# Rotation tables made in pieces during the recurrent phase and reloaded from device memory

## The chip, the cores and the metric

The kernel runs on one core of a Trainium2 chip. The metric is device time in microseconds (us) of one execution; the time before is the median of three. PE is TensorE (PEld its weight loads), DVE is VectorE, ACT is ScalarE, POOL is GpSimd, and SP is SyncE, which here only issues transfers.

## The reference, cut to what matters

One residual block over 2048 positions of width 1024: a norm, one projection to eight groups of 1024 columns, a recurrent branch and an attention branch over 8 heads, a merge by gates, an output projection and a final norm. The change touches the rotation of queries and keys by position, which concerns the first 32 of each head's 128 dimensions (16 frequencies, two halves).

```python
def apply_partial_rope(t, cos, sin):
    tf = t.astype(jnp.float32)
    half = ROT_DIM // 2
    x1 = tf[..., :half]
    x2 = tf[..., half:ROT_DIM]
    return jnp.concatenate([x1 * cos - x2 * sin, x2 * cos + x1 * sin, tf[..., ROT_DIM:]], axis=-1)
...
    inv_freq = ROPE_THETA ** (-jnp.arange(0, ROT_DIM, 2, dtype=jnp.float32) / ROT_DIM)
    ang = positions.astype(jnp.float32)[..., None] * inv_freq
    cos = jnp.cos(ang)[:, :, None, :]
    sin = jnp.sin(ang)[:, :, None, :]
...
        proj = h @ w_in[l]
        x_rnn, z_rnn, q, k, v, z_attn, g_r, g_a = jnp.split(proj, IN_SPLITS, axis=-1)
...
        qh = apply_partial_rope(q.reshape(B, S, N_HEADS, HEAD_DIM), cos, sin)
        kh = apply_partial_rope(k.reshape(B, S, N_HEADS, HEAD_DIM), cos, sin)
```

## The kernel before, in words

The positions are worked in two halves, f = 0 and 1, each of 1024 positions (two banks of 512, a tile being 128 columns of the projection by 512 positions). In each half come first the norm and the operands of the projection, with the values; then 28 pairs of column blocks are projected by Strassen's scheme (`strassen`): seven products of twelve 128 x 512 matmuls each, into PSUM tiles X (two of them), Z, W, V and Y (one each). Every matmul is three in float32 parts, hi and lo. A product `prod` takes its weight block S, split into hi and lo. In half 0 the block is made on the spot: SP loads raw blocks R (ring of five), DVE adds and subtracts them (L255 to L263), ACT writes hi (L200), POOL writes lo (L160), ACT's queue stores the result to memory (sD), and S is a ring of seven. In half 1 SP only loads it back (L288, 512 KB). The last product of a pair, into V, runs behind the first one of the next pair. Finished tiles are evicted through `done`: ACT or DVE (L418) writes them to an SBUF tile.

`prod` counts the products in `n_prod`. Code that should come some products later is put under a count in `late` or `after_prod`, and `prod` runs what is due; this gives the program's order. A planner then orders each engine's instructions, ahead of the run, from that order and its own estimate of when each is ready, so that an instruction can come earlier on its engine than its place in the program.

The pairs of a half form two phases. In the recurrent phase (buffers `rp`) eight pairs feed the recurrence (`recurrent`: steps tap, taps, split, gates, sigmoids, decay and so on to store, L735 to L834), and between them run pairs whose gates are evicted to a ring of three tiles "ev" and stored (`gate_pairs`), and two plain pairs. In the rotary phase (buffers `qp`) the rotation's tables are made, half 0 loads and normalises x for the next half (L468 to L478) and half 1 works out the residual gate, then two rotated pairs (one of queries, one of keys) and the remaining plain pairs run. A rotated pair holds the 32 rotated dimensions of all heads. Its four tiles go through `rotated`: eviction to t0 (three such in half 0, five in half 1), shuffle of the halves to t1 on DVE (L903), t0 times the cosine table Ct on POOL (L904), t1 times the signed sine table St on DVE (L905), the sum on DVE (L906), and four stores on SP (L909). Plain tiles are stored by SP too (L933).

`rotary_tables` makes Ct and St, each 128 x 1024, at the start of the rotary phase. It loads the half's positions, 8 per partition (`pi`, L838), and multiplies them by 16 frequencies to a tile `an` of 128 x 128. In 25 small DVE operations it brings the angles to within one turn by subtracting multiples of 2 pi in 8 and 5 parts (L849 to L853), makes the cosine's angle `co` a quarter turn further (L857, L858) and clips both (L860). Two ACT sines follow (L861). Then, for each bank and each of co and an, a DVE copy repeats the 4 x 8 x 16 values (`rep`, L868, one buffer), four PE transposes turn them (L870) to a PSUM tile pg (two of them, shared with the recurrent gates and the norm's transposes), and ACT (Ct, L874) or DVE (St, with a sign, L876) evicts 512 columns of the table. All on-chip; nothing of it goes to memory.

After both halves comes the attention, whose order is written out by hand, and which the change leaves alone.

Of the kernel before, what the change touches and what calls it, by code (L numbers as in the profile page):

```python
# [10 lines left out]
F32 = mybir.dt.float32  # L11
F32R = mybir.dt.float32r
BF16 = mybir.dt.bfloat16
I32 = mybir.dt.int32
AF = mybir.ActivationFunctionType
ALU = mybir.AluOpType
# [4 lines left out]
P = 128  # L21
# [3 lines left out]
NB = 4  # L25
CH = 512
H = 8
KH = KT // 2
HALF = 1024
# [5 lines left out]
FILL = (3.6, 3.1)  # L35
MORE = 0.8
NEG = 1e30

KV = 4

# [5 lines left out]
K_ID, K_QM, K_SG, K_IF, K_M23, K_M1, K_REP = 0, 128, 132, 133, 261, 773, 1029  # L46
# [4 lines left out]
def constants():  # L51
# [10 lines left out]
    old, prev, diag = q4, (d <= 0) + q4, np.where(d >= 0, 1 + q4, 0)  # L62
    add = np.array([NEG, 0.0, -math.log(2.0)])
    cst[:, K_M23 : K_M23 + 512] = add[np.concatenate([old, old, prev, diag], axis=1)]
# [6 lines left out]
def split_const(v, bits, n):  # L71
    out = []
    r = np.longdouble(v)
    for _ in range(n):
        m, e = math.frexp(float(r))
        q = math.floor(m * 2 ** bits) / 2 ** bits
        c = math.ldexp(q, e)
        out.append(c)
        r = r - np.longdouble(c)
    return out  # L80


TWO_PI = 8 * np.arctan(np.longdouble(1))
# [3 lines left out]
def decoder_block(ctx, tc, x, c, positions, g_norm, w_mod, b_mod, w_in, b_gate, conv_w, conv_b,  # L87
                  w_a, b_a, w_x, b_x, lam, w_out_rnn, w_out_attn, w_o, g_final, cst, out):
    nc = tc.nc
    cnt = [0]  # L90

    def T(pool, shape, dt, tag, **kw):
        cnt[0] += 1
        return pool.tile(shape, dt, tag=tag, name=f"{tag}_{cnt[0]}", **kw)
# [3 lines left out]
    def scratch(name, shape):  # L98
        return nc.dram_tensor(name, shape, F32, kind="Internal").ap()
# [10 lines left out]
    oT = scratch("oT", [D, S])  # L110
    meT = scratch("meT", [D, S])
    gateD = scratch("gateD", [1, D])

    sD = scratch("sD", [28 * 7, P, 2, KH, P])

# [20 lines left out]
    cs = T(cp, [P, N_CST_A], F32, "cs")  # L136
    ident = cs[:, K_ID : K_ID + P]
# [68 lines left out]
    n_prod, late, after_prod = [0], {}, {}  # L206
# [205 lines left out]
    def total(dst, ps, u, perm=lambda ap: ap):  # L412

        with tc.high_priority():
            if u is None:
                nc.scalar.activation(dst, perm(ps[:]), AF.Copy)
            else:
                nc.vector.tensor_tensor(dst, perm(ps[:]), perm(u[:]), ALU.add)  # L418
# [20 lines left out]
    def wcol(c0, n=P):  # L439
        return w_in[0, :, c0 : c0 + n]  # L440
# [17 lines left out]
    pg = pools.open("pg", bufs=2, space=PSUM)  # L458
# [107 lines left out]
    pt = T(pg, [P, CH], F32, "pg")  # L566
# [30 lines left out]
    for j in range(4):  # L597
# [3 lines left out]
        with ExitStack() as order:  # L601
            for ins in pm_ins[-1:] + gs_ins[-2:-1] + acc_ins[-1:]:
                order.enter_context(tc.issue_after(ins))
            for q in range(2):
                t = w_m[q, j]
# [227 lines left out]

        strassen(rp, f, ("r", m), [wcol(m * P), wcol(D + m * P)], done)  # L834

    def rotary_tables(qp, f):
        pi = T(qp, [P, 2, 4], I32, "pi")
        nc.sync.dma_start(pi[:], positions[0].rearrange("(n j r) -> j n r", n=NB, r=4)[:, 2 * f : 2 * f + 2, :])  # L838
        pf = T(qp, [P, 8], F32, "pf")
        nc.vector.tensor_copy(pf[:], pi[:].rearrange("p n r -> p (n r)"))  # L840
        an = T(qp, [P, 8, 16], F32, "an")
        nc.vector.tensor_tensor(
            an[:], pf[:].unsqueeze(2).broadcast_to([P, 8, 16]),
            cs[:, K_IF : K_IF + 128].rearrange("p (b f) -> p b f", f=16), ALU.mult)
        anf = an[:].rearrange("p b f -> p (b f)")
        kk = T(qp, [P, 128], F32, "kk")
        magic = 1.5 * 2.0 ** 23
        for per, bits, n in ((TWO_PI * 4096, 7, 8), (TWO_PI, 11, 5)):
            nc.vector.tensor_scalar(kk[:], anf, float(1 / per), None, ALU.mult)  # L849
            nc.vector.tensor_scalar(kk[:], kk[:], magic, None, ALU.add)  # L850
            nc.vector.tensor_scalar(kk[:], kk[:], -magic, None, ALU.add)
            for cc in split_const(per, bits, n):
                nc.vector.scalar_tensor_tensor(anf, kk[:], -cc, anf, ALU.mult, ALU.add)  # L853
        lim = 3.1415925
        co = T(qp, [P, 8, 16], F32, "co")
        cof = co[:].rearrange("p b f -> p (b f)")
        nc.vector.tensor_scalar(kk[:], anf, math.pi / 2, -float(TWO_PI), ALU.is_gt, ALU.mult)  # L857
        nc.vector.scalar_tensor_tensor(cof, anf, math.pi / 2, kk[:], ALU.add, ALU.add)  # L858
        for v in (anf, cof):
            nc.vector.tensor_scalar(v, v, lim, -lim, ALU.min, ALU.max)  # L860
            nc.scalar.activation(v, v, AF.Sin)  # L861
        Ct = T(qp, [P, HALF], F32, "Ct")
        St = T(qp, [P, HALF], F32, "St")
        for q in range(2):
            for src, dst in ((co, Ct), (an, St)):
                pt = T(pg, [P, 4, P], F32, "pg")
                rep = T(qp, [P, 4, 8, 16], F32, "rep", bufs=1)
                nc.vector.tensor_copy(rep[:], src[:, 4 * q : 4 * q + 4, :].unsqueeze(2).broadcast_to([P, 4, 8, 16]))  # L868
                for r in range(4):
                    nc.tensor.transpose(pt[:, r, :], rep[:, r].rearrange("p a b -> p (a b)"), ident)  # L870
                dv = dst[:, q * CH : (q + 1) * CH]
                pv_ = pt[:].rearrange("p r j -> p (r j)")
                if src is co:
                    nc.scalar.activation(dv, pv_, AF.Copy)  # L874
                else:
                    nc.vector.tensor_scalar(dv, pv_, cs[:, K_SG : K_SG + 1], None, ALU.mult)  # L876
        return Ct, St

    swap = [(i + 16) % 32 for i in range(32)]
# [60 lines left out]
    def gate_pairs(ep, f):  # L940
        for m in range(0, KT, 2):
            for base, dst, b0 in ((5 * D, zaT, None), (6 * D, grT, C_BG), (7 * D, gaT, C_BG + 8)):
                def gate(i, j, ps, u, m=m, dst=dst, b0=b0):
                    n = 2 * f + j
                    t = T(ep, [P, CH], F32, "ev", bufs=3)
                    v = ps
                    if u is not None:
                        v = t
                        total(t[:], ps, u)
                    if b0 is None:  # L950
                        sg = T(ep, [P, CH], F32, "sg", bufs=1)
# [33 lines left out]
    for f in range(2):  # L985
        if f:
            pools.close("xp")
            vx = pools.open("vx", bufs=1)
            x1 = load_x(hp, 3, "T", 14)
        values_half(f, x1)  # L990
        pools.close("vx")
        plain = plain_pairs(f)
        rp = pools.open("rp", bufs=1)
        plain_pool[0] = rp
        plain_at[0] = lambda: T(rp, [P, CH], F32, "ev", bufs=3)
        bigr = reset_rows(rp, f)
        gates = gate_pairs(rp, f)
        if f:
            output_weights()

        n = 0
        for m in range(KT):
            recurrent(rp, bigr, f, m)
            for _ in range(1 + (m % 4 > 0)):
                next(plain if n % 6 == 3 else gates)
                n += 1
        last_product()
        finish_late()
        pools.close("rp")
        qp = pools.open("qp", bufs=1)  # L1010
        plain_pool[0] = qp
        plain_at[0] = lambda: T(qp, [P, CH], F32, "t0", bufs=NT0[f])

        touch = [T(qp, [P, CH], F32, tag, bufs=n) for tag, n in (("t0", NT0[f]), ("t1", 2), ("u1", 1), ("u2", 2), ("u3", 1))]
        tabs = rotary_tables(qp, f)
        if f:
            residual_gate(qp)
        else:
            xp = pools.open("xp", side="right", bufs=1)
            x0 = load_x(xp, 2, "x", 2)  # L1020
            norm_x(xp, x0)
        rotated_pairs(qp, f, *tabs)
        for n, _ in enumerate(plain, 3):
            if n == 5 and f == 0:

                for p in range(7):
                    late.setdefault(n_prod[0] + p + 1 + (p > 0), []).append(lambda p=p: next_even(p))
        last_product()
        finish_late()
        for n in sorted(after_prod):  # L1030
            run_late(n)
        pools.close("qp")
# [36 lines left out]
    class Head:  # L1069
# [531 lines left out]
```

## Time and profile before

| | before |
|---|---|
| runs | 2332.69, 2337.65, 2343.75 us |
| median | 2337.65 us |
| profiled execution | 2338.7 us, mean PE clock 0.983 |
| its span | 2336.9 us |
| recurrent phase, half 0 and half 1 | about 148 to 650 us, 875 to 1335 us |
| rotary phase, half 0 and half 1 | about 650 to 775 us, 1335 to 1455 us |

The page of the profile gives busy time by engine over the span; a window gives the same for a stretch, with the clock granted to PE as a share of full speed; the timeline lists instructions in order with their idle time before and what ended it. The phases' limits are read from where the lines of `recurrent` and `rotated_pairs` begin and end. The costliest transfers of these phases are the split weight blocks' stores and loads:

```profile
sD<-S ACTq DMA_DIRECT2D x196, 512.0 KB, 4.2
R<-in_w_in_dram SPq DMA_DIRECT2D x136, 256.0 KB, 3.9
zaT<-ev SPq DMA_DIRECT2D x32, 256.0 KB, 4.5
```

### The profile page before, as it was taken

The numbers are of one execution on the slowest core, as the hardware profiler recorded it, in microseconds if no ns is written. First come the engines' busy times: TensorE is split into PE (matmuls) and PEld (weight loads), VectorE is DVE, ScalarE is ACT, GpSimd is POOL, SyncE is SP. The second block draws the span as 40 slices with busy tenths as digits, with TensorE's granted clock in tenths as the row PEclk, the third lists the DMA queues.
The fourth block names the chain that finished last, engine by engine and source line by source line (L and its number), as shares of the span: only waits on it lengthen the run. The fifth ranks groups of instructions, "written<-read, shape, count | busy, mean of one in ns | idle before, by whom it ended". The sixth has DMA issues, their size and how long they took to land.

```text
span 2336.9 us, 34037 instructions
## 1 busy us (share of the span) xinstructions
PE 2246.0 (96%) x11461; PEld 1872.0 (80%) x11461; DVE 1347.5 (58%) x2442; ACT 1206.0 (52%) x2391; POOL 952.1 (41%) x734
## 2 busy tenths in 40 slices
PE   8998999899989999999999999999999898989998
PEld 4996777677777998787888877888889797978887
DVE  4737666756676534544434472366666777658443
ACT  4636656665643635555444411567768787634111
POOL 2456556665545533332211120446565656433000
PEclk9999999999999999999999999999999999999999
DMA  7375777676778759999677778989987887799532
GB/s 263 108 237 205 277 265 262 239 243 246 242 246 268 227 174 327 311 325 322 227 231 225 234 250 269 301 245 266 279 254 247 236 245 238 221 310 281 179 122 95
DMA packets 427284, 569.21 MB, mean 244 GB/s; under 512 B 71942, under 2 KB 292834, under 8 KB 426084
## 3 DMA queue, kind: packets, MB, share of 16 engines
q1 hardware_dynamic: 389268, 447.27, 62.2%
q10 hardware_dynamic: 37648, 119.70, 13.3%
q8 instruction: 91, 1.49, 0.3%
q14 instruction: 85, 0.70, 0.1%
q0 software_dynamic: 192, 0.05, 0.0%
HBM read 355.08 MB, written 211.82 MB: 243 GB/s over the span
## 4 chain that ended last, share of the span: by engine, by line
PE 50%; DMA 8%; DVE 4%; ACT 3%; issue 3%; POOL 2%; SPq 1%; ACTq 0%; POOLq 0%; DVEq 0%
PE pj L146 11%; PE pq L146 7%; PE X L146 6%; PE V L146 6%; PE o L146 4%; PE sc L146 4%; PE Z L146 3%; PE W L146 3%; PE Y L146 2%; PE pT L1217 1%; DMA wD<-s 1%; PE pT L1230 1%; PE pg L146 1%; DMA vraw<-vN 1%; DVE yl L163 1%
## 5 line engine op out<-in xcount | busy, mean ns | idle before, releaser
L146 PE MATMUL pj<-yh,S 128*128 128x512 f32 x1024 | 372.0, 408 | 6.1 <-DMA S<-wD 3.2
L146 PE MATMUL V<-T,S 128*128 128x512 f32 x1344 | 334.3, 397 | 12.0 <-ACT t L809 5.2
L160 POOL TENSOR_TENSOR S<-R,S 128x512 fp32r<-128x512 f32 x168 | 241.8, 1455 | 253.8 <-ACT S L200 79.2
L146 PE MATMUL X<-T,S 128*128 128x512 f32 x1344 | 332.4, 395 | 1.2 <-ACT t L888 1.2
L146 PEld LDWEIGHTS V<-T,S 128*128 128x128 f32 x1344 | 252.6, 189 | 75.9 <-ACT t L809 7.2
L146 PEld LDWEIGHTS X<-T,S 128*128 128x128 f32 x1344 | 252.4, 188 | 61.8 <-ACT t L888 2.1
L146 PEld LDWEIGHTS pj<-yh,S 128*128 128x128 f32 x1024 | 195.6, 191 | 44.0 <-DVE fg L1424 3.6
L146 PE MATMUL pj<-yl,S 128*128 128x512 f32 x512 | 203.0, 397 | 0.0
L1133 ACT ACTIVATE pp<-pp,st 128x256 f32<-128x256 f32 (+3 forms) x256 | 133.9, 524 | 113.4 <-DVE st L1132 112.7
L146 PE MATMUL W<-T,S 128*128 128x512 f32 x672 | 174.1, 404 | 0.0
L146 PE MATMUL Y<-T,S 128*128 128x512 f32 x672 | 168.6, 398 | 2.1 <-DVE t L418 2.1
L146 PE MATMUL Z<-T,S 128*128 128x512 f32 x672 | 167.4, 397 | 0.0
L146 PEld LDWEIGHTS W<-T,S 128*128 128x128 f32 x672 | 130.3, 194 | 32.4 <-issue 0.9
L146 PEld LDWEIGHTS Y<-T,S 128*128 128x128 f32 x672 | 127.0, 190 | 33.3 <-DVE t L418 2.5
L146 PEld LDWEIGHTS Z<-T,S 128*128 128x128 f32 x672 | 127.5, 190 | 30.2
L160 POOL TENSOR_TENSOR S<-s,S 128x512 fp32r<-128x512 f32 x84 | 114.9, 1369 | 77.7 <-ACT S L200 55.0
L163 DVE TENSOR_TENSOR ptl<-pT,pth 128x384 fp32r<-128x384 f32 (+1 forms) x160 | 97.8, 628 | 64.8 <-ACT pth L154 62.6
L1197 ACT ACTIVATE pp<-pp,M 128x256 f32<-128x256 f32 (+3 forms) x256 | 117.9, 523 | 8.7 <-DVE M L1321 8.6
L1132 DVE CUSTOM_DVE_ANT_0 pp<-sc,msk 128x256 f32<-128x256 f32 (+3 forms) x256 | 105.1, 449 | 30.0 <-PE sc L146 27.2
L779 DVE SCALAR_TENSOR_TENSOR xc<-xr,par,xc 128x512 f32<-128x512 f32 x96 | 84.8, 883 | 56.5 <-ACT xc L773 55.6
L160 POOL TENSOR_TENSOR kq<-kraw,kq 128x512 fp32r<-128x512 f32 (+1 forms) x64 | 101.1, 1590 | 22.9 <-ACT kq L154 22.9
L160 POOL TENSOR_TENSOR vh<-vraw,vh 128x256 fp32r<-128x256 f32 (+1 forms) x64 | 67.2, 1050 | 105.1 <-ACT vh L154 99.4
(358 smaller groups left out, 4697.7 us busy)
## 6 DMA issues: line engine op xcount, KB each, us to landing
sD<-S ACTq DMA_DIRECT2D x196, 512.0 KB, 4.2
S<-sD SPq DMA_DIRECT2D x196, 512.0 KB, 5.0
S<-wD SPq DMA_DIRECT2D x99, 512.0 KB, 5.5
R<-in_w_in_dram SPq DMA_DIRECT2D x136, 256.0 KB, 3.9
wD<-s ACTq DMA_DIRECT2D x64, 256.0 KB, 5.5
T<-in_w_mod_dram SPq DMA_DIRECT2D x8, 1024.0 KB, 11.5
vN<-ev SPq DMA_DIRECT2D x64, 128.0 KB, 2.7
zaT<-ev SPq DMA_DIRECT2D x32, 256.0 KB, 4.5
```

What stands on the lines that cost most here:

```text
L146: last_mm[0] = nc.tensor.matmul(o, lhsT=l, rhs=r, start=st, stop=sp, **kw).ins
L160: nc.gpsimd.tensor_tensor(o, i, h.bitcast(F32), ALU.subtract)
L163: return nc.vector.tensor_tensor(o, i, h.bitcast(F32), ALU.subtract).ins
L779: nc.vector.scalar_tensor_tensor(xc, xr[:, i : i + CH], cw(i), xc, ALU.mult, ALU.add)
L1132: nc.vector.tensor_tensor_reduce(pdst, s_ps, mask, 1.0, 3e38, ALU.add, ALU.min, m_)
L1133: nc.scalar.activation(pdst, pdst, AF.Exp, bias=m_, scale=-1.0, accum_out=l_)
L1197: nc.scalar.activation(pp, pp, AF.Copy, scale=w)
L1217: nc.tensor.transpose(pt[:, c0 + j * P : c0 + (j + 1) * P], pp[i][:, k * P : (k + 1) * P], ident)
L1230: nc.tensor.transpose(pt[:, c * P : (c + 1) * P], pp[:, half * P : (half + 1) * P], ident)
```

## The change: what it does

The tables are computed by the same operations, but registered in `after_prod` during the recurrent phase of the same half: the positions' load 24 products after that phase's start, the angle steps one or a few operations per product behind it, the sines last. Each of the four pieces (bank q, cosine or sine) has its place in PIECES: the copy, the transposes two products later, eviction and store one after that. Copy and evicted piece live in the ring "ev" that the gates and plain pairs of this phase use. The piece is stored (256 KB, SP) to a new internal tensor `tabD` in device memory. In the rotary phase `load_tables` fetches Ct and St (512 KB each, SP) in the place where the positions were loaded. So each half issues four stores and two loads more; the arithmetic and its count stay.

```diff
+TABLES = 24
+PIECES = (58, 79, 110, 131)
...
+    tabD = scratch("tabD", [2, 2, P, HALF])
...
-    def rotary_tables(qp, f):
-        pi = T(qp, [P, 2, 4], I32, "pi")
...
+    def rotary_tables(rp, f):
+        v = {}
+        def angles():
+            pi = T(rp, [P, 2, 4], I32, "pi")
+            nc.sync.dma_start(pi[:], positions[0].rearrange("(n j r) -> j n r", n=NB, r=4)[:, 2 * f : 2 * f + 2, :])
+            v["pi"] = pi
+            for tag in ("an", "kk", "co"):
+                v[tag] = T(rp, [P, 8, 16], F32, tag)
...
+        def sines():
+            for tag in ("an", "co"):
+                nc.scalar.activation(flat(tag), flat(tag), AF.Sin)
+        def piece(q, i):
+            def repeat():
+                src = v[("co", "an")[i]]
+                v["rep"] = T(rp, [P, 4, 8, 16], F32, "ev", bufs=3)
+                nc.vector.tensor_copy(v["rep"][:], src[:, 4 * q : 4 * q + 4, :].unsqueeze(2).broadcast_to([P, 4, 8, 16]))
+            def turn():
+                v["pt"] = T(pg, [P, 4, P], F32, "pg")
+                for r in range(4):
+                    nc.tensor.transpose(v["pt"][:, r, :], v["rep"][:, r].rearrange("p a b -> p (a b)"), ident)
+            def store():
+                t = T(rp, [P, CH], F32, "ev", bufs=3)
+                pt = v["pt"][:].rearrange("p r j -> p (r j)")
+                if i == 0:
+                    nc.scalar.activation(t[:], pt, AF.Copy)
+                else:
+                    nc.vector.tensor_scalar(t[:], pt, cs[:, K_SG : K_SG + 1], None, ALU.mult)
+                nc.sync.dma_start(tabD[f, i, :, q * CH : (q + 1) * CH], t[:])
+            return repeat, turn, store
+        at_, base = TABLES, n_prod[0]
+        for fn in (angles, None, products, *reduce(TWO_PI * 4096, 7, 8), *reduce(TWO_PI, 11, 5), quarter, sines):
+            if fn:
+                after_prod.setdefault(base + at_, []).append(fn)
+            at_ += 1
+        for x, (q, i) in enumerate((q, i) for q in range(2) for i in range(2)):
+            for d, fn in zip((0, 2, 3), piece(q, i)):
+                after_prod.setdefault(base + PIECES[x] + d, []).append(fn)
+    def load_tables(qp, f):
         Ct = T(qp, [P, HALF], F32, "Ct")
         St = T(qp, [P, HALF], F32, "St")
-        for q in range(2):
-            for src, dst in ((co, Ct), (an, St)):
...
+        for i, t in enumerate((Ct, St)):
+            nc.sync.dma_start(t[:], tabD[f, i])
         return Ct, St
...
         gates = gate_pairs(rp, f)
+        rotary_tables(rp, f)
...
-        tabs = rotary_tables(qp, f)
+        tabs = load_tables(qp, f)
```

More of the change, by code (lines that the diff above doesn't have):

```diff
@@ L834, in recurrent @@
         strassen(rp, f, ("r", m), [wcol(m * P), wcol(D + m * P)], done)
-    def rotary_tables(qp, f):
-        pi = T(qp, [P, 2, 4], I32, "pi")
[L838 to L846, printed above, removed]
-        magic = 1.5 * 2.0 ** 23
[L848 to L861, printed above, removed]
@@ new lines, in rotary_tables, with products, reduce, multiple @@
+    def rotary_tables(rp, f):
[6 more added lines that the diff above has]
+                v[tag] = T(rp, [P, 8, 16], F32, tag)
+        def products():
+            pf = T(rp, [P, 8], F32, "pf")
+            nc.vector.tensor_copy(pf[:], v["pi"][:].rearrange("p n r -> p (n r)"))
+            nc.vector.tensor_tensor(
+                v["an"][:], pf[:].unsqueeze(2).broadcast_to([P, 8, 16]),
+                cs[:, K_IF : K_IF + 128].rearrange("p (b f) -> p b f", f=16), ALU.mult)
+        flat = lambda tag: v[tag][:].rearrange("p b f -> p (b f)")
+        magic = 1.5 * 2.0 ** 23
+        def reduce(per, bits, n):
+            def multiple():
+                anf, kk = flat("an"), flat("kk")
+                nc.vector.tensor_scalar(kk, anf, float(1 / per), None, ALU.mult)
+                nc.vector.tensor_scalar(kk, kk, magic, None, ALU.add)
+                nc.vector.tensor_scalar(kk, kk, -magic, None, ALU.add)
+            def subtract(ccs):
+                anf, kk = flat("an"), flat("kk")
+                for cc in ccs:
+                    nc.vector.scalar_tensor_tensor(anf, kk, -cc, anf, ALU.mult, ALU.add)
+            ccs = split_const(per, bits, n)
+            return [multiple] + [lambda i=i: subtract(ccs[i : i + 3]) for i in range(0, n, 3)]
+        def quarter():
+            anf, kk, cof = flat("an"), flat("kk"), flat("co")
+            nc.vector.tensor_scalar(kk, anf, math.pi / 2, -float(TWO_PI), ALU.is_gt, ALU.mult)
+            nc.vector.scalar_tensor_tensor(cof, anf, math.pi / 2, kk, ALU.add, ALU.add)
+            lim = 3.1415925
+            for a in (anf, cof):
+                nc.vector.tensor_scalar(a, a, lim, -lim, ALU.min, ALU.max)
+        def sines():
[27 more added lines that the diff above has]
+                after_prod.setdefault(base + PIECES[x] + d, []).append(fn)
@@ L862, in rotary_tables @@
+    def load_tables(qp, f):
         Ct = T(qp, [P, HALF], F32, "Ct")
         St = T(qp, [P, HALF], F32, "St")
-        for q in range(2):
-            for src, dst in ((co, Ct), (an, St)):
[L866 to L876, printed above, removed]
+        for i, t in enumerate((Ct, St)):
+            nc.sync.dma_start(t[:], tabD[f, i])
```

## The prediction, made before the changed kernel was run

> **What bounds the kernel now.** I began with the page's totals: the span, and how much of it TensorE (PE) works.
>
> ```profile
> span 2336.9 us, 34037 instructions
> PE 2246.0 (96%) x11461; PEld 1872.0 (80%) x11461; DVE 1347.5 (58%) x2442; ACT 1206.0 (52%) x2391; POOL 952.1 (41%) x734
> ```
>
> PE is busy for all but 2336.9 − 2246.0 = 90.9 us. The change removes no work from PE, so it can only win PE's idle time, and the time PE loses at a lower granted clock, in the stages that it touches. So I cut the span into stretches: the recurrent phase of half 0, its rotary phase (two stretches and two stalls inside them), then the same two phases of half 1. The columns are start and end, length, busy time and instructions of PE, PEld, DVE, ACT and POOL, PE's clock, DMA share, GB/s.
>
> ```profile
> 400.00:500.00 100.00, 93.59 (x390) 74.10 (x389) 66.63 (x70) 58.67 (x99) 61.64 (x43) 0.97 0.69 241
> 650.00:700.00 50.00, 44.23 (x193) 35.40 (x191) 36.56 (x82) 21.62 (x39) 21.69 (x16) 0.97 0.72 232
> 700.00:750.00 50.00, 46.33 (x192) 36.45 (x191) 34.40 (x46) 13.16 (x23) 27.06 (x20) 0.97 0.85 261
> 686.00:690.00 4.00, 3.84 (x12) 3.20 (x13) 2.83 (x6) 0.00 (x0) 0.00 (x0) 0.57 0.75 166
> 709.00:714.00 5.00, 4.69 (x14) 3.73 (x14) 4.97 (x7) 0.66 (x2) 5.00 (x4) 0.66 0.89 289
> 1080.00:1180.00 100.00, 100.00 (x431) 80.69 (x431) 48.01 (x62) 53.79 (x84) 20.12 (x16) 1.00 0.74 246
> 1335.00:1400.00 65.00, 65.00 (x284) 50.87 (x283) 44.64 (x86) 10.12 (x17) 10.90 (x7) 1.00 0.81 263
> 1400.00:1450.00 50.00, 48.05 (x207) 38.46 (x206) 10.46 (x16) 3.03 (x5) 1.80 (x1) 1.00 0.88 287
> ```
>
> The two halves are two different cases. Half 1 makes its tables between 1335 and 1400 us with PE busy for every microsecond: there they already cost PE nothing but their transposes. In half 0's rotary phase PE idles 5.77 + 3.67 = 9.44 us of 100. The timeline of PE says which waits these are (start, duration, engine, line, tiles; in brackets the idle time before and what ended it).
>
> ```profile
> 675.10 0.66 PE L870 MATMUL pg<-cs,rep 128*128 128x128 f32 x4 [0.73 <-DVE rep L868]
> 686.16 0.94 PE L870 MATMUL pg<-cs,rep 128*128 128x128 f32 x4 [5.04 <-DVE rep L868]
> 700.58 0.66 PE L489 MATMUL pg<-cs,x 128*128 128x128 f32 x4 [0.41 <-DVE St L876]
> 709.31 4.62 PE L146 MATMUL Y<-T,S 128*128 128x512 f32 x12 [2.06 <-DVE t L418]
> 726.29 3.04 PE L146 MATMUL X<-T,S 128*128 128x512 f32 x12 [1.20 <-ACT t L888]
> 1361.70 0.60 PE L870 MATMUL pg<-cs,rep 128*128 128x128 f32 x4
> 1362.06 1.42 PE L146 MATMUL V<-T,S 128*128 128x512 f32 x5
> 1413.66 3.04 PE L146 MATMUL V<-T,S 128*128 128x512 f32 x12 [1.95 <-DMA S<-sD]
> ```
>
> 0.73 + 5.04 + 0.41 + 2.06 + 1.20 = 9.44: these five are all of it. The 5.04 us are a transpose that PE took in its turn before DVE had written the repeated angles. After it the clock is 0.57 over 4 us, (1 − 0.57) × 4 = 1.7 us of lost work; after the 2.06 us stall it is 0.66 over 5 us, 1.7 us again. What half 0's phase can give is 9.44 + 3.4 = 12.9 us.
>
> **What goes from the rotary phases.** The rows of DVE and POOL show why the copy was late, and what else the tables hold up.
>
> ```profile
> 653.05 1.13 SPq L838 DMA_DIRECT2D pi<-in_positions_dram  x1
> 657.84 0.73 DVE L903 STREAM_SHUFFLE t<-t 128x512 f32<-128x512 f32 x1
> 679.51 1.29 POOL L904 TENSOR_TENSOR t<-t,Ct 128x512 f32<-128x512 f32 x1
> 679.61 3.42 DVE L478 TENSOR_SCALAR x<-x,ss 128x1024 f32<-128x1024 f32 x2
> 682.95 1.75 DVE L263 TENSOR_TENSOR s<-R,s 128x512 f32<-128x512 f32 x1
> 684.62 1.48 DVE L868 COPY rep<-an 128x512 f32<-128x512 f32 x1
> 706.79 1.74 DVE L906 TENSOR_TENSOR t<-t,t 128x512 f32<-128x512 f32 x1 [1.19 <-POOL t L904]
> 708.57 0.69 DVE L418 TENSOR_TENSOR t<-Y,u 128x512 f32<-128x512 f32 x1
> ```
>
> The copy of 684.62 stood behind 3.42 us of normalisation and 1.75 us of operand sums. Without tables there no PE instruction waits for it: the stalls of 0.73, 5.04 and 0.41 us and the 1.7 us of clock go, 7.9 us together. This is the sure part, the lower bound of the gain.
>
> The 2.06 us stall is indirect. Its eviction at 708.57 waited in DVE's queue behind the addition of 706.79, and that one for POOL's product. The rotation ran late: the first shuffle was at 657.84, the first product with Ct at 679.51, 21.7 us later, because Ct did not exist. With Ct loaded, the four rotated tiles are worked off as they are evicted, and DVE has 25 small operations, four copies and two evictions fewer in this phase. I take this stall and its 1.7 us of clock as won too: 7.9 + 3.8 = 11.7 us. The 1.20 us (a free t0 buffer, behind ACT) I leave. Bounds 7.9 and 12.9; I choose near the top because the indirect stall starts from the same lateness.
>
> By the Trainium skill, page "TensorE: Matmul & The Clock Gate", section "What's actually happening", the clock halves after at least one idle window of about 3.4 us; a stall of 2.06 us alone would then cost none, and the gain would be 10.0 in place of 11.7 us. The row of 0.66 behind that stall speaks against it.
>
> In half 1, 1.95 us before the product at 1413.66 were a wait for a weight load, while PE had no other idle time in these 115 us. SP issues the stores of the rotated tiles in one queue with the weight loads, and a store whose tile is late holds the loads behind it:
>
> ```profile
> SPq L909 <- DVE t L906: 15.2, 8, 6.9
> S<-sD SPq DMA_DIRECT2D x196, 512.0 KB, 5.0
> ```
>
> That is half 0's count of SP's waits at these stores (15.2 us in eight, the longest 6.9). Earlier rotation shortens them. I take 1.0 us of the 1.95 (bounds 0 and 1.95).
>
> **What moves at no price.** The 16 transposes of a half go over to the recurrent phase one for one; where PE does not wait a group of four costs 0.36 us of PE's time (1361.70 to 1362.06), 1.4 us per half on either side: net nothing. The two loads of Ct and St (512 KB each) stand on SP where the positions' load stood (653.05), ahead of the loads of x and of the weights. Loads of that size take 5.0 us to land (row above), so Ct is there about 658 us, when the first shuffle ends; the cover is that shuffle, and without it POOL, which runs in order, would hold the splits behind its first product for up to 5 us. Weight loads behind them lose some 1 to 2 us, covered by the rings of loaded blocks. Half 1's recurrent phase takes its share in DVE's free half (48.01 of 100 us busy, PE 100.00): nothing; if that cover failed it would be the same price as in half 0 next.
>
> **What it costs in half 0's recurrent phase.** In the changed order the 25 angle operations of half 0 stand not spread out but in the first recurrent pair, on DVE between the reset row (before, 161.6 us) and the decay's companion, the operand sum of 181.14 and the evictions of V behind it. The sines with their table load stand on ACT ahead of that pair's last weight splits and the first gate's sigmoid. Their durations, and what waits in this place:
>
> ```profile
> 650.00:700.00 50.00, 7.64 (x21) 0.97 0.72 232
> 1335.00:1385.00 50.00, 5.56 (x21) 1.00 0.84 282
> 658.74 0.29 DVE L842 TENSOR_TENSOR an<-pf,cs 128x128 f32<-128x128 f32 x1
> 672.05 1.28 ACT L861 ACT_TABLE_LOAD   x1
> 673.35 0.31 ACT L861 ACTIVATE an<-an 128x128 f32<-128x128 f32 x1
> 174.07 2.64 DVE L779 SCALAR_TENSOR_TENSOR xc<-xr,par,xc 128x512 f32<-128x512 f32 x2 [2.26 <-ACT xc L773]
> 181.14 1.76 DVE L263 TENSOR_TENSOR s<-R,s 128x512 f32<-128x512 f32 x1 [1.52 <-POOL S L160]
> 199.88 3.03 PE L146 MATMUL V<-T,S 128*128 128x512 f32 x12 [1.92 <-ACT S L200]
> 223.17 1.22 PE L146 MATMUL pg<-xh,gh 128*128 128x512 f32 x2 [5.82 <-ACT xh L154]
> ```
>
> The first two rows are DVE's time on the 21 operations that touch kk, in half 0 and half 1: 7.64 and 5.56 us. The other four are no longer than the 0.29 us one; with them I count 6.5 to 8.5 us of DVE (an estimate). DVE stood idle 2.26 + 1.52 = 3.8 us in the stretch where they land, so DVE comes out about 7.7 − 3.8 = 3.9 us late at the sum of 181.14, which feeds the weight splits on ACT. ACT adds 1.28 + 2 × 0.31 = 1.9 us. PE already waits 1.92 us for such a split at 199.88, so there is no slack: the worst is 3.9 + 1.9 = 5.8 us, with a lowered clock behind it 7.5. But PE stalls again at 223.17, 5.82 us for the split of that same chain of steps; a chain delayed on PE's side meets it with less stall left. I take 3 us (bounds 0 and 7.5), under the middle because of that later stall.
>
> The Trainium skill, page "ScalarE: Activation LUTs", section "What ACT_TABLE_LOAD costs", adds a drain of about 1.38 us to the load of 1.28. The rows show the next activation 1.30 us after the load's start, so no drain; by the page this front would cost 1.4 us more.
>
> The four pieces of half 0 come later: copy, two products on (5.6 us, at the 2.8 us that twelve matmuls take) the transposes, one on the eviction and a 256 KB store on SP. The rep and the piece take two turns in the ring of three eviction tiles. A store on SP waits for its eviction with the loads of raw weight blocks behind it; five raw tiles cover that. A piece costs PE nothing while DVE is under two products late; over that it costs what the old place did, 5.04 + 1.7 = 6.7 us. Half 0's recurrent phase has DVE at 67% and PE idling 6.4 of 100 us already, so lateness occurs. I take 1 us for the four (bounds 0 and 27).
>
> **Sum.** −11.7 − 1.0 + 3 + 1 = −8.7 us. The profiled execution took 2338.7 us (span and 1.8 us around it): 2330.0. It stands 1.05 us above the median of the three runs, so the forecast for the median is 2329 us, 0.4% less. The case's own range is 2325 to 2334. About 0.5% (11.7 us, so 2326 to 2349) is what a measurement of this kernel can tell from no change.
>
> **Rivals.**
>
> *More than that.* The whole 12.9 and 1.95 us come, and the front costs nothing, because the later stall of 5.82 us absorbs all of it: 2338.7 − 14.8 − 1.05 = 2322.9 us. For it: the 17% of DVE's time that goes from half 0's phase. Against: the 199.88 wait without slack.
>
> *The change does not free the rotation.* The order behind the shuffle is again set by DVE and POOL in queue (L906 behind L904), not by Ct: only 7.9 us come back, the front takes 5.8 of them, half 1 gives nothing: 2338.7 − 2.1 − 1.05 = 2335.5. For it: L906 took 1.74 us, its 1.19 us wait for POOL behind it, at a time when Ct had long existed.
>
> *Slower: the pieces' transposes stall PE in the recurrent phase.* The stall of 686.16 returns where PE meets transposes in its order before DVE has made the copy. It decides when DVE runs more than two products (5.6 us) behind. With the full front (7.5) and two of half 0's pieces at 6.7 it is 7.5 + 13.4 − 11.7 = +9.2, 2347; with all four +22.6, 2360; between them 2353. For it: the six-microsecond waits as at 223.17, which show that this phase does run a chain late. Against: the copy is one operation of 0.4 to 1.5 us, and the planner places it before its due time.
>
> **How the numbers follow.** Forecast 0.42, more 0.29, not freed 0.14, slower 0.15. Of the forecast's case I put 0.09 under 2326, so faster is 0.29 + 0.09 = 0.38; of the slower case 0.10 lies over 2349, so slower is 0.10 and the rest, 0.52, is the same. The range goes from 2320 (the second case less its spread) to 2344: what it leaves out is most of the slower case (0.12) and an end of the second (0.06).
>
> **What would show it.** Right: in half 0's rotary phase no wait of PE for rep or St and 53 to 60% DVE; the first product with Ct some 2 us behind the first shuffle instead of 21.7; the clock near 1.00. The front: the wait for S at the first pair's end grown from 1.92 us to 4 to 7, and that for xh after it shrunk. The pieces: PE's waits at the four transposes of the recurrent phase, none over 1 us. Wrong: stalls of 5 us at these transposes, PE waiting for POOL's split because POOL stands at its first product for Ct, or half 1's recurrent phase no longer full.

## The result and the profile after

| | before | changed |
|---|---|---|
| median of 8 runs | 2337.35 us | 2349.38 us |
| lowest to highest | 2332.69 to 2343.75 | 2341.04 to 2350.73 |
| ratio (95% interval) | | 1.0041 (1.0027 to 1.0055) |
| profiled execution | 2338.7 us | 2341.04 us |

The changed kernel is slower by 0.4%; the median lies above the range that was given. The profiled execution is the fastest of its eight, and the other seven (2348 to 2351) have no trace. So the whole loss is read from the medians and the ratio; what a single place loses can only be read from this one trace, and is less sure.

The page of the changed kernel shows as much PE time as before:

```profile
span 2339.3 us, 34073 instructions
PE 2240.9 (96%) x11461; PEld 1867.0 (80%) x11461; DVE 1355.0 (58%) x2442; ACT 1203.7 (51%) x2390; POOL 952.9 (41%) x734
```

A total hides where time went. Both kernels run the same 392 Strassen products, so the start of the n-th product on PE (counted from the first pair's) can be set side by side. In the table, worked out from PE's matmuls in both traces, the third number is how far the changed kernel is behind, in us:

```
product  place                                 before    after   behind
      0  half 0, recurrent phase starts        147.62   147.60    -0.0
     14                                        188.04   191.96    +3.9
     21                                        211.54   221.02    +9.5
     28                                        241.32   248.77    +7.5
    161  half 0, rotary phase                  662.12   669.11    +7.0
    175                                        716.55   710.73    -5.8
    182                                        737.53   739.64    +2.1
    196  half 1, recurrent phase starts        875.19   877.32    +2.1
    217                                        936.58   947.10   +10.5
    224                                        961.26   968.68    +7.4
    245                                       1022.75  1030.44    +7.7
    266                                       1084.72  1095.12   +10.4
    350  half 1, rotary phase starts          1332.07  1343.64   +11.6
    385  its last pairs                       1436.14  1443.63    +7.5
    end of the span                           2336.92  2339.26    +2.3
```

Three places lose most: the fronts of both recurrent phases, some 7.5 us in half 0 and 5.3 in half 1 (from 2.1 to 7.4), and, within half 0's rotary phase, products 175 to 182, where 7.9 us of a gain of 12.8 are given back. The attention behind it all, which the change leaves alone, was 5 us quicker in this execution; the eleven other kernels' traces have 1.7 to 6.6 us of the same, so it is the one trace of before that is slow there.

The same code does not take the same time in every trace. By product starts, half 0's recurrent phase as it was before is 2.6 us quicker in the trace of e5_half1_only and 2.6 slower in that of e11_before_apart (both below); half 0's rotary phase as it was before is 2.3 and 3.3 us slower in those of e2_front_extra and e5_half1_only; and products 196 to 224 of half 1 as before are 2.5 and 3.1 us quicker in those of e10_half0_values and e11_before_apart. So each size of the table is good to some 3 us, and the front of half 1 costs 5.3 us against the trace of before, but 7.8 and 8.4 against these two.

The windows of before at the two fronts, and then of the changed kernel there, in half 0's rotary phase and in half 1's (columns as in the prediction):

```profile
200.00:250.00 50.00, 43.96 (x176) 34.53 (x177) 36.34 (x35) 31.93 (x53) 33.02 (x23) 0.93 0.63 224
900.00:950.00 50.00, 48.35 (x200) 38.34 (x200) 29.95 (x35) 33.06 (x52) 20.51 (x16) 0.97 0.89 309
```

```profile
200.00:250.00 50.00, 39.79 (x153) 31.23 (x152) 39.27 (x40) 32.75 (x55) 29.20 (x20) 0.86 0.59 209
900.00:950.00 50.00, 44.92 (x181) 35.57 (x180) 35.91 (x50) 31.16 (x48) 17.75 (x13) 0.93 0.77 262
650.00:700.00 50.00, 48.33 (x206) 38.28 (x205) 35.63 (x61) 20.72 (x39) 28.77 (x20) 1.00 0.94 315
700.00:750.00 50.00, 44.75 (x183) 35.30 (x182) 32.09 (x42) 14.04 (x24) 28.25 (x20) 0.93 0.89 267
1400.00:1450.00 50.00, 50.00 (x216) 40.23 (x215) 8.84 (x14) 5.37 (x9) 0.00 (x0) 1.00 0.92 284
```

At each front PE loses 3.4 to 4.2 us and the granted clock is lower by 0.04 to 0.07, over 50 us another 2 to 3.5 us. The rotary phase wins in its first 50 us and loses in the second. PE's timeline names the waits:

```profile
178.39 2.07 PE L151 MATMUL V<-T,S 128*128 128x512 f32 x4 [2.29 <-DVE xr L423]
207.80 5.02 PE L151 MATMUL V<-T,S 128*128 128x512 f32 x12 [5.91 <-ACT S L205]
231.05 1.22 PE L151 MATMUL pg<-xh,gh 128*128 128x512 f32 x2 [4.31 <-ACT xh L159]
679.35 3.02 PE L151 MATMUL V<-T,S 128*128 128x512 f32 x12 [1.67 <-DVE t L423]
718.00 3.06 PE L151 MATMUL V<-T,S 128*128 128x512 f32 x12 [1.74 <-DVE t L423]
728.46 5.49 PE L151 MATMUL X<-T,S 128*128 128x512 f32 x12 [3.51 <-ACT t L938]
918.40 3.07 PE L151 MATMUL V<-T,S 128*128 128x512 f32 x12 [0.49 <-DVE ev L423]
933.03 5.49 PE L151 MATMUL V<-T,S 128*128 128x512 f32 x12 [4.59 <-DVE ev L423]
```

The wait for the split block S went from 1.92 to 5.91 us, an eviction of V by DVE (L423, the old L418) is late by 2.29 us, and the chain's later wait for xh fell from 5.82 to 4.31. Why DVE is so late: its time on the 21 operations with kk, in the first pairs of the halves, then two of these operations with no POOL instruction beside them, and two beside POOL's:

```profile
155.00:192.00 37.00, 14.24 (x21) 0.95 0.59 208
895.00:920.00 25.00, 13.12 (x21) 1.00 0.77 277
```

```profile
169.53 0.21 DVE L867 TENSOR_SCALAR kk<-kk 128x128 f32<-128x128 f32 x1
170.66 0.28 DVE L872 SCALAR_TENSOR_TENSOR an<-kk,an 128x128 f32<-128x128 f32 x1
```

```profile
186.77 1.35 POOL L801 TENSOR_TENSOR gi<-gi,xc 128x512 f32<-128x512 f32 x1
186.99 1.20 DVE L879 TENSOR_SCALAR kk<-an 128x128 f32<-128x128 f32 x1
188.07 1.29 POOL L165 TENSOR_TENSOR xl<-xc,xh 128x512 fp32r<-128x512 f32 x1
188.23 1.28 DVE L880 SCALAR_TENSOR_TENSOR co<-an,kk 128x128 f32<-128x128 f32 x1
```

In the rotary phases the same 21 took 7.64 and 5.56 us. Here they cost twice that, because an operation of 0.2 to 0.3 us that meets a POOL instruction ends just behind POOL's: 188.19 behind 188.12, 189.51 behind 189.36. The Trainium skill, page "SBUF — State Buffer", section "SBUF: two separate sides", has the rule: a POOL operation that reads SBUF and a DVE operation that has two inputs in SBUF or runs in a two-port mode share one port pair, and whichever starts first holds it by an exclusive lock for its whole instruction, while the other blocks. The row of L880, with two inputs, agrees, at some 1.0 us; L879 has one input and is as late, and whether it ran in a two-port mode no row shows.

### The profile page after: what moved, and what is told of

Read it like the earlier page. It is cut to its first block, busy times and chain, and to the rows that moved or that the text cites. A ratio compares the mean times of both kernels' runs of the same rounds, so it can differ in the third digit from the quotient of the medians.

```text
span 2339.3 us, 34073 instructions
## 1 busy us (share of the span) xinstructions
PE 2240.9 (96%) x11461; PEld 1867.0 (80%) x11461; DVE 1355.0 (58%) x2442; ACT 1203.7 (51%) x2390; POOL 952.9 (41%) x734
## 3 DMA queue, kind: packets, MB, share of 16 engines
q10 hardware_dynamic: 37648, 119.70, 13.2%
## 4 chain that ended last, share of the span: by engine, by line
PE 65%; DVE 10%; DMA 10%; ACT 6%; issue 4%; POOL 2%; SPq 1%; ACTq 1%; DVEq 0%; POOLq 0%
PE pj L151 12%; PE X L151 10%; PE V L151 10%; PE pq L151 8%; PE W L151 5%; PE Z L151 5%; PE o L151 4%; PE Y L151 4%; PE sc L151 4%; DMA R<-in_w_in_dram 2%; POOL S L165 2%; PE pg L151 2%; PE pT L1268 1%; DVE xc L784 1%; PE pT L1281 1%
## 5 line engine op out<-in xcount | busy, mean ns | idle before, releaser
L151 PE MATMUL pj<-yh,S 128*128 128x512 f32 x1024 | 367.3, 403 | 5.5 <-ACT S L159 3.0
L151 PE MATMUL V<-T,S 128*128 128x512 f32 x1344 | 339.6, 402 | 28.1 <-DVE ev L423 12.2
L784 DVE SCALAR_TENSOR_TENSOR xc<-xr,par,xc 128x512 f32<-128x512 f32 x96 | 84.7, 883 | 49.5 <-ACT xc L778 48.8
```

The lines of the kernel that those rows point to most:

```text
L151: last_mm[0] = nc.tensor.matmul(o, lhsT=l, rhs=r, start=st, stop=sp, **kw).ins
L784: nc.vector.scalar_tensor_tensor(xc, xr[:, i : i + CH], cw(i), xc, ALU.mult, ALU.add)
```

## The experiments

Each ratio compares an experiment with executions of the kernel before that were measured beside it, whose median was between 2334.22 and 2337.57 us. So two experiments are compared by their ratios and intervals rather than by their bare times.

### Where the angle work stands

In `e1_held` each angle step is tied behind the last evictions on DVE and ACT, so that the planner can't draw it ahead:

```diff
+    def held(fn):
+        def run():
+            with tc.issue_after(last_dve[0]), tc.issue_after(last_act[0]):
+                fn()
+        return run
...
-                after_prod.setdefault(base + at_, []).append(fn)
+                after_prod.setdefault(base + at_, []).append(held(fn) if fn is not angles else fn)
```

> The changed kernel, but each angle step is tied behind the last DVE and ACT eviction of its own product, so the 25 angle operations and the sines stand spread over products 26 to 35 of the recurrent phase and can't be drawn to its first pair. Theory F (the loss is the angle work ahead of the first pairs' evictions of V; by the traces it cost 7.4 us in half 0 and 5.3 us in half 1): some 9 to 13 us come back, 2336 to 2341 us, PE's waits for S and for V in the first three pairs are those of before. Rival P (the pieces, their ring and stores cost it): stays at 2347 to 2351. Rival W (the angle work costs wherever it stands): stays too, with the stalls now in the fourth and fifth pair.

Measured: 2333.33 us, ratio to before 0.9990 (0.9976 to 1.0004). The front of half 0 is gone but for 0.4 us of S:

```profile
202.34 4.59 PE L151 MATMUL V<-T,S 128*128 128x512 f32 x12 [2.31 <-ACT S L205]
225.64 1.22 PE L151 MATMUL pg<-xh,gh 128*128 128x512 f32 x2 [4.76 <-ACT xh L159]
```

The time lies under the range that either case gave. Against the changed kernel it is 0.5% by the ratios, some 12 us, and the intervals are apart: within the 9 to 13 of theory F, and as much as the trace of the changed kernel shows for both fronts (7.5 and 5.3 us). So theory F holds and rival P falls. W holds in part: by product starts, 4.8 us are lost in half 0 between products 42 and 49, right behind the spread angle work.

`e2_front_extra` is the opposite test: the kernel before, plus an unused second set of angle steps and sines at the changed kernel's place (a call of `extra_angles(rp, f)` behind `gate_pairs`, with the steps of `rotary_tables` and no pieces).

> The kernel before, with its rotary phases as they were, and besides them a second, unused set of angle operations and sines in the recurrent phase at the changed kernel's place: the front alone, without pieces, stores and loads. Theory F: 10 to 13 us slower than before, 2347 to 2350 us. Rival P: 2337 to 2340 us.

Measured: 2352.06 us, ratio 1.0066 (1.0048 to 1.0084). This is 2 us over theory F's range. The front alone costs all that the change costs, and by the medians a little more (the intervals overlap). The same two waits are there, without a piece, a store or a load:

```profile
206.35 5.17 PE L148 MATMUL V<-T,S 128*128 128x512 f32 x12 [6.00 <-ACT S L202]
937.13 5.04 PE L148 MATMUL V<-T,S 128*128 128x512 f32 x12 [4.59 <-DVE ev L420]
```

Its trace is 6.5 us behind after the front of half 0, 5.4 more after that of half 1, and 4.7 more by product 266, where the changed kernel too lost 3. There the order on DVE differs. Before, and then in the changed kernel, the eviction of V and the product that waits for ACT's root:

```profile
1042.08 0.68 DVE L418 TENSOR_TENSOR ev<-V,u 128x512 f32<-128x512 f32 x1
1043.75 0.69 DVE L813 TENSOR_TENSOR t<-t,gi 128x512 f32<-128x512 f32 x1 [0.99 <-ACT t L809]
```

```profile
1051.66 0.69 DVE L818 TENSOR_TENSOR t<-t,gi 128x512 f32<-128x512 f32 x1 [1.32 <-ACT t L814]
1052.27 0.68 DVE L423 TENSOR_TENSOR ev<-V,u 128x512 f32<-128x512 f32 x1
```

The eviction now stands behind an instruction that waits, and PE's wait for V at this place is 1.42 us instead of none. Why the planner turned the two was not tried. But e11_before_apart, whose half 1 is as before and keeps the old order, loses 2.6 us between products 224 and 266 too, with a wait of 0.76 us at this place, and e10_half0_values 1.1; so this order isn't shown to cost the 3 us.

`e3_no_sine` takes the sine's table load out of the front (`AF.Copy` in place of `AF.Sin`, so the tables hold angles).

> The changed kernel with a copy on ACT in place of each sine, so the values of the tables are not sines and the sine's table load falls away; all else the same. If the front's price is ACT's table load (1.3 us a half and what is queued behind it): 4 to 8 us come back, 2341 to 2345. If it is DVE's 25 operations: within 2 us of the changed kernel, 2347 to 2351.

Measured: 2342.89 us, ratio 1.0028 (1.0015 to 1.0042): in the range for ACT's load, and 6.5 us under the changed kernel's median, but the intervals overlap and the ratios differ by only 0.13% (3 us). The traces don't settle it either. Half 0's front is 4.9 us here against 7.5, but it is 5.2 in the trace of e4_t1_three (below), which has the sines; half 1's is 5.5 against 5.3, and the two profiled executions are equal (2341.1 and 2341.0). Whether ACT's load has a share is left open. Most of the front stays without it.

`e5_half1_only` keeps half 0 as before and moves half 1's tables alone.

> Half 0 as in the kernel before (tables in its rotary phase), half 1 as in the changed one. It puts a price on half 1 by itself. Theory F: the front of half 1 costs what its trace showed (5.3 us, and 2.9 more around 1050 us), the four groups of transposes 1.4, and 4.1 come back in its rotary phase: 4 to 8 us slower than before, 2341 to 2345. Rival Z (half 1 has free engines and takes the tables at no price, as the prediction said): 2335 to 2338, not slower than before.

Measured: 2343.12 us, ratio 1.0035 (1.0018 to 1.0053). Half 1 is slower by itself, though PE was busy there for nearly all of the time before (48.35 of 50 us at the front, 100 of 100 further on): rival Z, the prediction's own step, falls. In its trace products 196 to 224 lose 4.4 us, with a wait of PE for V of 4.58 us where the changed kernel has 4.59.

### What held the rotary phase of half 0

After the rows of PE above, DVE and POOL in the changed kernel, first at the rotation's start, then ahead of the stalls:

```profile
668.56 0.76 DVE L953 STREAM_SHUFFLE t<-t 128x512 f32<-128x512 f32 x1
669.39 1.30 POOL L954 TENSOR_TENSOR t<-t,Ct 128x512 f32<-128x512 f32 x1 [4.84 <-DMA St<-tabD]
712.07 3.46 DVE L955 TENSOR_TENSOR t<-t,St 128x512 f32<-128x512 f32 x2
715.46 1.77 DVE L956 TENSOR_TENSOR t<-t,t 128x512 f32<-128x512 f32 x1
717.26 0.69 DVE L423 TENSOR_TENSOR t<-V,u 128x512 f32<-128x512 f32 x1
```

The first product with Ct now comes 0.8 us behind the start of the first shuffle. The row names the load of St, but what came last was the shuffle: the product overwrites the tile that the shuffle reads, and starts 0.07 us behind the shuffle's end (668.56 + 0.76 = 669.32), while Ct, issued at 662.03 and landed 6.4 us later, was there at 668.46. But the eviction of V at 717.26 stands behind products and sums that take 1.7 to 1.8 us each beside POOL, and the eviction of X into t0 (L938) waits for such a sum. Two kernels try the buffers: `e4_t1_three` has three t1 in half 0, `e6_t0_four` four t0.

> The changed kernel with three buffers of t1 in half 0's rotary phase instead of two. Theory R (in the rotary phase the gain was given back because a shuffle waits for a free t1, whose stores stand in SP's queue, and the evictions of V and X behind it stall PE 1.74 and 3.51 us): 3 to 8 us come back, 2341 to 2346. Rival (the rotation is held by DVE and POOL in turn, not by the buffers): within 2 us of the changed kernel, 2347 to 2351.

> The changed kernel with four buffers of t0 in half 0's rotary phase instead of three. Theory R2 (what was given back there, 3.5 us at the eviction of X and the lowered clock behind it, is the wait for a free t0): 3 to 8 us come back, 2341 to 2346. Rival (another buffer only shifts the stall to the next eviction in DVE's queue, as three t1 did): within 2 us of the changed kernel, 2347 to 2351.

Measured: 2348.63 us, 1.0048 (1.0030 to 1.0065), and 2346.07 us, 1.0046 (1.0032 to 1.0060): neither differs from the changed kernel (1.0041) by its ratio, though the second median lies just between the two ranges. The wait moves, and is as long; first three t1, then four t0:

```profile
707.20 4.78 PE L151 MATMUL V<-T,S 128*128 128x512 f32 x12 [5.25 <-DVE t L423]
```

```profile
704.94 5.45 PE L151 MATMUL V<-T,S 128*128 128x512 f32 x12 [5.10 <-DVE t L423]
```

So one more buffer of either kind does not free the rotation: theories R and R2 fall.

### The angle work at the end of the values

`e7_values` calls the angle work behind the last values of each half, with its two results kept in the constant pool; the pieces stay as they are.

```diff
+        with tc.issue_after(last_dve[0]), tc.issue_after(last_act[0]):
+            nc.vector.tensor_copy(pf, pi.rearrange("p n r -> p (n r)"))
...
         for m in (3, 0, 1, 2):
             for _ in values(vx, m, ws if m == 3 else load_wv(m), n1):
                 next(odd, None)
+        angle_tables(f)
```

> The pieces as in the changed kernel, but the angle work (25 operations and the sines) behind the operand sums at the end of each half's values, where PE is full and DVE and ACT are idle for more than half of the time. The tile for the warming matmuls is 128 columns wide, read four times, to make room. Theory F: no front in either recurrent phase and none of the 4.8 us that the spread angle work cost in e1_held; 2327 to 2333 us. Rival (the price is paid by whoever makes the angles): 2338 or more, with PE stalling at the end of the values.

Measured: 2327.05 us, ratio 0.9963 (0.9950 to 0.9976), faster than both kernels. Part of the work is no cheaper there: eight operations, beside four of POOL's, take 6.53 us (first its timeline, then a window). But PE is full beside it:

```profile
114.12 6.53 DVE L734 SCALAR_TENSOR_TENSOR an<-t,an 128x128 f32<-128x128 f32 x8
```

```profile
100.00:150.00 50.00, 50.00 (x421) 49.96 (x420) 25.22 (x49) 16.91 (x29) 17.42 (x14) 1.00 0.44 128
```

`e8_values_rings` adds both larger rings.

> e7_values with four t0 and three t1 in half 0's rotary phase. If the rotation's buffers hold what is left there (7.4 us given back in e1_held between products 178 and 181): 4 to 8 us under e7_values. If only one in-order queue of DVE holds it: within 2 us of e7_values.

Measured: 2328.56 us, 0.9969 (0.9958 to 0.9979), as without them. Its DVE shows what holds V when no buffer does, and the wait of PE behind it:

```profile
691.27 3.07 DVE L940 TENSOR_TENSOR t<-t,St 128x512 f32<-128x512 f32 x2
694.27 0.71 DVE L938 STREAM_SHUFFLE t<-t 128x512 f32<-128x512 f32 x1
695.48 1.75 DVE L940 TENSOR_TENSOR t<-t,St 128x512 f32<-128x512 f32 x1
697.15 0.68 DVE L423 TENSOR_TENSOR t<-V,u 128x512 f32<-128x512 f32 x1
```

```profile
697.88 4.62 PE L151 MATMUL V<-T,S 128*128 128x512 f32 x12 [4.56 <-DVE t L423]
```

The eviction stands in DVE's queue behind a run of the rotation's products and shuffles, a burst. `e9_apart` thins the burst out, with a plain pair between the two rotated ones:

```diff
-        rotated_pairs(qp, f, *tabs)
-        for n, _ in enumerate(plain, 3):
+        for _ in rotated_pairs(qp, f, *tabs):
+            next(plain)
+        for n, _ in enumerate(plain, 5):
```

> e7_values with a plain pair between the two rotated pairs (and one behind the second) in both halves. In e8_values_rings more buffers moved the stall of half 0's rotary phase to an eviction of V that stood on DVE behind a burst of shuffles, products and sums. Theory Q (the burst of eight rotations on DVE's in-order queue, slowed beside POOL, gives back the gain): with the rotated pairs apart the 6 to 8 us that were given back come, 2319 to 2323 us. Rival (four rotations are enough to fill DVE's queue): as e7_values, 2325 to 2329.

Measured: 2323.70 us, ratio 0.9949 (0.9929 to 0.9969): between the two ranges, and the interval overlaps that of e7_values, so the medians don't settle it. The same 80 us as a window of the changed kernel, as a window of this one, and then the only long wait of this one's PE in that stretch:

```profile
655.00:735.00 80.00, 73.08 (x303) 57.36 (x302) 59.18 (x92) 28.55 (x52) 47.45 (x33) 0.96 0.90 288
```

```profile
655.00:735.00 80.00, 78.89 (x339) 63.27 (x338) 57.31 (x94) 29.65 (x53) 49.45 (x35) 1.00 0.95 303
```

```profile
716.17 3.06 PE L151 MATMUL V<-T,S 128*128 128x512 f32 x12 [1.04 <-DVE t L423]
```

PE does 5.8 us more work in the stretch, at full clock. By product starts this phase wins 15.0 us against before (from +1.8 at product 161 to −13.2 at 175) and gives almost none of it back by product 189 (−13.0). Its profiled execution is the fastest of its six, but the phase behaves the same way in every trace of the other order: the five with loaded tables, three t0 and two t1, and the rotated pairs together (the changed kernel, e1_held, e3_no_sine, e7_values, e10_half0_values) each win 12.8 to 14.4 us by product 175 and give 6.8 to 8.1 back by product 182. So the traces speak for theory Q; that it shortens the whole execution isn't shown.

Two controls. `e10_half0_values` is e7_values with half 1 as before; `e11_before_apart` is the kernel before with e9_apart's order of pairs.

> e7_values in half 0, and half 1 as in the kernel before. If moving half 1's tables wins something once the angles are out of the way (by e7_values' trace 2.6 us there, of it 1.95 the wait for a weight block): 1 to 4 us slower than e7_values, 2328 to 2331. If half 1 is free either way: as e7_values within 1 us.

> The kernel before with the same order of pairs as e9_apart, its tables still in the rotary phases. If the order of pairs wins by itself, it is as fast as e9_apart, 2321 to 2326 us. If the tables' stalls have to go first (the copies late for the transposes, no Ct for the first product), it wins at most the 3.8 us of the stall of 2.06 us and its clock: 2333 to 2339 us.

Measured: 2331.97 us, 0.9981 (0.9968 to 0.9994), and 2341.39 us, 1.0010 (0.9997 to 1.0023), 2 us over the higher of its two ranges. The interval of the first overlaps that of e7_values, so what half 1 wins by itself is not shown in time. By the traces, half 1's wait for a weight block is there again when its tables stay in the rotary phase (first fence). The order of pairs alone wins nothing, and there the transposes still wait for the copies (second):

```profile
1410.19 4.59 PE L151 MATMUL V<-T,S 128*128 128x512 f32 x12 [2.23 <-DMA S<-sD]
```

```profile
682.12 1.11 PE L870 MATMUL pg<-cs,rep 128*128 128x128 f32 x4 [2.98 <-DVE rep L868]
693.23 0.66 PE L870 MATMUL pg<-cs,rep 128*128 128x128 f32 x4 [2.41 <-DVE rep L868]
```

## Why the prediction was wrong, step by step

**The rotary phase of half 0.** The 11.7 us were won: up to product 175 the changed kernel gains 12.8, of which 1.4 are the transposes that moved. The step of this part that failed is "The 1.20 us (a free t0 buffer, behind ACT) I leave". That wait did not stay: with the rotation early and PE quicker, an eviction of X into t0 waited 3.51 us, one of V ahead of it 1.74, and the clock fell behind them, 7.9 us in all. The third case had the place (DVE and POOL in queue, not Ct), and took it for a bound on what comes back rather than for a new wait. That the burst on DVE is what holds it, the traces of e8_values_rings and e9_apart support. DVE's share, foretold at 53 to 60%, stayed at 68% (35.63 + 32.09 of 100 us): the tables' work is gone, but the eight products with St and the eight sums of half 0 took 20.8 us in place of 16.4, in 100 us of which POOL was busy for 57.0 instead of 48.8.

**The front of half 0.** The place, the order and the waits were as foretold (S from 1.92 to 5.91 us, xh shrunk). The term was mis-sized: 3 us taken, 7.5 in the trace, which is the upper bound that the text gave (5.2 and 7.1 in the traces of the same front in e4_t1_three and e6_t0_four). Two steps made it small. DVE's price was carried over from the rotary phases, 6.5 to 8.5 us, without asking how busy POOL is in the new place; it was over 13. And the later stall was to absorb more than half: xh's wait gave back 1.5 us.

**Half 1's recurrent phase.** "Half 1's recurrent phase takes its share in DVE's free half ...: nothing" is the step with the wrong kind of argument. DVE's 48% is an average over 100 us that begin at 1080; the 25 operations fell on one pair at 900 to 920 us, on the chain that frees the only buffer of V. It cost 5.3 us or more, and e5_half1_only puts half 1 at +0.35% by itself. The text had set the price for a failed cover ("the same price as in half 0 next") and named a recurrent phase that is no longer full as a sign of being wrong, but did not count it in the sum or in a rival.

**The pieces.** 1 us was taken for half 0. In the four kernels where no angle work disturbs it (e7_values to e10_half0_values), half 0's recurrent phase, with the same pieces, falls 5.4, −0.4, 2.3 and 3.4 us behind, 1.4 of it transposes. That is some 1.3 us for the pieces in the mean, in a phase that varies by more, so the term is neither shown nor refuted. Rival three's stall of 5 us at the transposes did not come: one of the changed kernel's, the third in half 0, made PE wait 1.76 us for its copy, over the 1 us that was allowed, and the others none. So the slower outcome came by its front in both halves and not by its pieces.

**The loads.** Ct was not there at about 658 us but at 668.46: its load was issued at 662.03, in a phase that began 7 us later than before, and took 6.4 us to land instead of 5.0. The cover that the text named, the first shuffle, held all the same: it ended at 669.32. So what ended POOL's 4.84 us was that shuffle, which had itself waited 2.97 us for ACT, and not a table. Whether the new wait of PE of 1.67 us at 679.35 comes from there isn't shown.

**Half 1's rotary phase** gave 4.1 us, 1.4 of them transposes, against 1.0 foretold; the 1.95 us wait for a weight block went altogether, and is there again (2.23 us) in e10_half0_values, whose half 1 is as before.

**The sum.** To product 385: +7.5 −0.5 −4.9 +5.3 +3.0 +1.2 −4.1 = +7.5 us, against −8.7. The terms are the front of half 0, its later pairs with the pieces, its rotary phase, then half 1's front, the stretch around 1050 us, its later pairs and its rotary phase. The ratio of 1.0041 is 9.6 us, the bare medians are 12 us apart; the rest is in no trace, since the other seven executions have none, and it stays open.

## What to carry to other kernels

Work that is moved out of a stalled stage has to be priced in the pair where the order puts it, beside the engines that run there, and not by its old durations or by an average load of the new stage; a planner that fills free slots will draw spread steps together unless each is tied to its place. Small elementwise steps belong where PE is full and their engine has no eviction to deliver. And when a stall is removed, the next one on the same queue can take back part of the gain, here 7 to 8 us of 13 to 14; thinning out the burst behind it kept the gain in the one trace that tried it.

## What the runs showed of the hardware

A DVE operation of 128 x 128 that takes 0.2 to 0.3 us took 1.2 to 1.3 beside a POOL instruction, one-input operations (L879) as well as two-input ones (L880). And the granted clock fell at a stall of 2.29 us (it ended at 178.39, the first long one of the recurrent phase), from 1.00 over the 3 us up to 178 to 0.57 over the 4 us behind it, in the windows of the changed kernel:

```profile
175.00:178.00 3.00, 1.10 (x5) 0.56 (x3) 2.96 (x3) 0.31 (x2) 3.00 (x3) 1.00 0.22 89
178.00:182.00 4.00, 3.61 (x10) 2.89 (x11) 3.86 (x9) 1.43 (x3) 2.22 (x2) 0.57 0.33 131
```
